# Conditioning products of a two-layer DiT as four column groups of 256 instead of two of 512, with the row turned by transposes

## The chip, the cores and the metric

One core of a Trainium2 chip. The metric is the time of one execution in device microseconds (us), as the median of several runs. Engines are called as in the profile: PE is TensorE's products, PEld its weight loads, DVE is VectorE, ACT ScalarE, POOL GpSimd, SP SyncE (whose queue issues most transfers).

## The reference, cut to what matters

A model of two layers with hybrid attention: 1024 tokens of 1024 features and 256 context rows. Every layer starts with a modulation whose three parts come from one product of a small vector with a wide matrix:

```python
def _modulate(x, cond, norm_g, w_ada, b_ada):
    mod = jax.nn.silu(cond) @ w_ada + b_ada
    shift, scale, gate = jnp.split(mod[:, None, :], 3, axis=-1)
    return rmsnorm(x, norm_g) * (1.0 + scale) + shift, gate

h, gate = _modulate(x, c, norm_g, w_ada, b_ada)
hc, gate_c = _modulate(xc, c_ctx[None, :], norm_g, w_ada, b_ada)
...
x = x + gate * (y @ w_out)
```

There are two vectors, `c` for the tokens and `c_ctx` for the context; `w_ada` is 1024 x 3072 in fp32, one for each layer. Shift and scale are wanted with the features on the partitions, the gate as a row.

## The kernel before, in words

All work on TensorE is products of 128 partitions. The large products take both factors as a high and a low part (three products each, lines L288 to L290); the conditioning is done in plain fp32.

`ada_third(wt, name, layer, third)` (from L400) computes one third of one layer's modulation: third 0 is shift, 1 is scale, 2 is gate. It runs over eight steps `kt` of 128 input features. A step loads 128 x 1024 of the matrix into a tile `wada` (SP's queue, six buffers) and makes two products on line L407. The weights on the array are `sil`, silu of the two vectors, padded with zeros to 32 columns; what streams through are the 512 columns of each half `c`. A product uses one group `g` of 32 columns of the array, and writes 32 partitions of the PSUM tile `acc[c]`. The group moves with the step, so each of the two PSUM tiles holds four partial sums, on its four groups of partitions:

```python
for c in range(2):
    g = 32 * ((kt + 2 * c) % 4)
    T_.matmul(acc[c][g:g + 32, :], sil[:, kt], w[:, c * 512:(c + 1) * 512], start=kt < 4, stop=kt >= 4)
```

ACT and DVE copy the two halves to a row in SBUF (`mrow`, L412). The four partial sums are then added up by another product with `fold`, a 128 x 2 matrix that has ones for each group's two real rows. For shift and scale the row is the weight, eight products of two columns give the features on the partitions (L433, `tps`), and DVE adds the bias into `modT` (L440) and, for scale, multiplies with the norm's weight (L443). For a gate `fold` is the weight, two products give a row (L419), DVE adds the bias `bada`, and a transfer writes it to memory (`GROW`), from where the output projection loads it.

Two of the six thirds are computed in the first stage: (layer 0, scale), while the first four blocks of x are normed (L457), turned (L481) and copied; and (layer 0, shift), between the first projections (`products`) and the turning of four more blocks (`cols_scaled`, L496). In the first of them line L488, ACT's scaling of the turned blocks into `hE`, waits for `modT`; L573 is ACT's cast of a weight `ws`. Around 65 to 150 us context columns are turned (L464, whose evictions are `hE` and `hf`, L467 to L473), queries and keys get their rope (`rope_split`: shuffle L315, POOL L316, DVE L317 and L318), and the values `vat` are projected (L656) and turned (L697); `qb` (L636) is a small bias for the first queries.

The other four thirds, in the order of `ADA_E1` = (0, gate), (1, shift), (1, scale), (1, gate), run in the second stage (`cond_gen`, from L706) beside the value projections (`main_gen`), whose weights are split into `whi` (ACT, L234) and `wlo` (DVE and POOL, L235). A `Filler` interleaves two generators: each `yield` tells how many us of TensorE's time it has issued, and after each step of the conditioning the other side may issue `FILL_E1` us. A scheduler then places the instructions of each engine; the order it gives is read from the lists under "The change".

Of the kernel before, what the change touches and what calls it, by code (L numbers as in the profile page):

```python
# [9 lines left out]
F32 = mybir.dt.float32  # L10
# [4 lines left out]
ALU = mybir.AluOpType  # L15
# [3 lines left out]
P = 128  # L19
D = 1024  # L20
NK = D // P
# [10 lines left out]
SM_COND, SM_GE, SM_GO, SM_SUB, SM_SINK, SM_LAM, SM_QG, SM_BE, SM_BO = 0, 16, 24, 32, 33, 41, 297, 300, 316  # L32
# [11 lines left out]
Q_BUFS_D, WO_V, WO_Y, YL_V = 2, 2, 5.0, 1  # L44
M_HALF = 2
POOL_MIX, POOL_Q = (0,), (8,)
# [51 lines left out]
def body(nc, tc, I, out, dbg=None):  # L98
    V, A, G, T_, SY = nc.vector, nc.scalar, nc.gpsimd, nc.tensor, nc.sync
# [11 lines left out]
    const = pool(top, "const", side="left")  # L111
# [15 lines left out]
    def s_ps():  # L127
        return psc.tile([P, 512], F32, tag="s", name="sps")

    def t_ps():  # L130
        return ptp.tile([P, 512], F32, tag="tp", name="tps")
# [5 lines left out]
    SY.dma_start(small, I["small"])  # L137
    consts = const.tile([P, P + 2], F32, name="consts")
    SY.dma_start(consts, I["ident"])
    ident, fold = consts[:, :P], consts[:, P:]  # L140
    modT = [const.tile([P, 16, 2], F32, name=f"modT{i}") for i in range(2)]
# [30 lines left out]
    GROW = spill("grow", [3, D])  # L172
# [11 lines left out]

    # ---- small helpers
    def rsqrt(v, n):
# [50 lines left out]

    # ---- interleaving of generators; what they yield is the tensor engine's time in us
    def run(gen):
# [45 lines left out]

    # ---- products
    def mm3(ps, lh, ll, rh, rl, first, last):
# [110 lines left out]

    # ---- conditioning
    def ada_third(wt, name, layer, third):  # L400
        acc = [s_ps() for _ in range(2)]
        for kt in range(NK):
            w = wt.tile([P, D], F32, tag="wada", name="wada", bufs=ADA_BUFS)
            SY.dma_start(w, I[name][kt * P:(kt + 1) * P, third * D:(third + 1) * D])
            for c in range(2):
                g = 32 * ((kt + 2 * c) % 4)
                T_.matmul(acc[c][g:g + 32, :], sil[:, kt], w[:, c * 512:(c + 1) * 512], start=kt < 4, stop=kt >= 4)  # L407
            yield 0.5
        split = (layer, third) == (0, 1)
        row = wt.tile([P, D], F32, tag="mrow", name="mrow", bufs=1)  # L410
        for c in range(2):
            (V.tensor_copy if c else A.copy)(row[:, c * 512:(c + 1) * 512], acc[c])  # L412
        if third == 2:
            b = wt.tile([2, D], F32, tag="bada", name="bada", bufs=1)
            SY.dma_start(b, I["b_gate"][layer])
            for c in range(2):
                cs_ = slice(c * 512, (c + 1) * 512)
                ps = t_ps()
                T_.matmul(ps[:2, :], fold, row[:, cs_], start=True, stop=True)  # L419
                V.tensor_tensor(b[:, cs_], ps[:2, :], b[:, cs_], ALU.add)  # L420
            if layer == 0:
                SY.dma_start(GROW[0:2], b)
            else:
                SY.dma_start(GROW[2:3], b[0:1])
        else:
            if split:
                yield 0.0
            nh = M_HALF if split else 1
            for i0 in range(0, 8, 8 // nh):
                n = 8 // nh  # L430
                ps = t_ps()
                for i in range(n):
                    T_.matmul(ps[:, 2 * i:2 * i + 2], row[:, (i0 + i) * P:(i0 + i + 1) * P], fold,  # L433
                              start=True, stop=True)

                def feat(off):
                    return small[:, off + i0:off + i0 + n].unsqueeze(2).to_broadcast([P, n, 2])

                dst = modT[layer][:, 8 * third + i0:8 * third + i0 + n]
                V.tensor_tensor(dst, ps[:, :2 * n].rearrange("p (i j) -> p i j", j=2),  # L440
                                feat((SM_BO if layer else SM_BE) + 8 * third), ALU.add)
                if third == 1:
                    V.scalar_tensor_tensor(dst, dst, 1.0, feat(SM_GO if layer else SM_GE), ALU.add, ALU.mult)  # L443
        yield 0.2
# [74 lines left out]

    # ---- even layer  # L520
    mark("start")
# [203 lines left out]

    # ---- window attention, the other queries and keys alongside
    mark("A")
# [122 lines left out]

    # ---- differential attention, the gates and the conditioning alongside
    mark("B")
# [155 lines left out]

    # ---- output projection, even; h of the odd layer
    def out_half(op, y, wo, x, gate, xn, c, kts):  # L1010
# [60 lines left out]

    # ---- odd layer
    LCH = CHUNKS[:2]
# [161 lines left out]

    # ---- neighbourhood attention, the gates alongside
    mark("D")
# [146 lines left out]

    # ---- latent attention
    mark("M")
# [92 lines left out]

    # ---- output projection, odd; final norm  # L1480
    mark("outO")
# [44 lines left out]
def layout(inp):  # L1526
    f = {k: np.asarray(v) for k, v in inp.items()}
    r = {}
# [40 lines left out]
    r["fg"] = f["final_norm_g"].reshape(1, D)  # L1569
    r["ident"] = np.concatenate([np.eye(P), np.tile(np.eye(32, 2), (4, 1))], axis=1).astype(np.float32)  # L1570
    r["flip"] = 8.0 * np.eye(P, dtype=np.float32)[::-1]
# [20 lines left out]
```

## Time and profile before

| what | us |
|---|---|
| median of 3 runs | 1714.09 |
| lowest and highest run | 1710.77 and 1715.72 |
| span of the profiled execution | 1716.7 |
| PE busy in it | 1622.0 (94%) |
| DVE, ACT, POOL busy | 1121.5, 780.7, 465.9 |
| DMA, mean over the span | 142 GB/s |

The profiled execution's own time is its span, 2.6 us above the median. A page of such a profile gives the busy time of each engine first; since PE's 94% is a mean over stages with different limits, the stages of the conditioning (from 11 us to 260 us) are shown apart in the rows below. In a row, "idle before <- releaser" names what ended the idle time just ahead of an instruction, and PEclk is the clock that TensorE was granted, as a share of full speed. A group such as "x8" holds instructions of one line that lie next to each other, with the time from the first start to the last end.

### The profile page before, as it was taken

The numbers are of one execution on the slowest core, as the hardware profiler recorded it, in microseconds if no ns is written. First come the engines' busy times: TensorE is split into PE (matmuls) and PEld (weight loads), VectorE is DVE, ScalarE is ACT, GpSimd is POOL, SyncE is SP. The second block draws the span as 40 slices with busy tenths as digits, with TensorE's granted clock in tenths as the row PEclk, the third lists the DMA queues.
The fourth block names the chain that finished last, engine by engine and source line by source line (L and its number), as shares of the span: only waits on it lengthen the run. The fifth ranks groups of instructions, "written<-read, shape, count | busy, mean of one in ns | idle before, by whom it ended". The sixth has DMA issues, their size and how long they took to land. (4 is left out here: it accounts for less than half of the span.)

```text
span 1716.7 us, 26624 instructions
## 1 busy us (share of the span) xinstructions
PE 1622.0 (94%) x9378; PEld 1359.4 (79%) x9378; DVE 1121.5 (65%) x2974; ACT 780.7 (45%) x1592; POOL 465.9 (27%) x388
## 2 busy tenths in 40 slices
PE   6988999999999989998989999999999999999997
PEld 3676668888887877887777798889788887888886
DVE  4583207878759887888677646352577666666586
ACT  4342105757646655655433323222466554545321
POOL 0252104545433222322322201120232223322110
PEclk9999999999999999999999999999999999999999
DMA  7446764243251423321754523558855345321362
GB/s 272 167 120 200 230 193 118 76 132 117 74 207 58 121 71 123 104 99 56 227 178 135 178 74 111 175 170 237 213 170 166 91 133 180 129 80 62 90 224 98
DMA packets 157155, 242.98 MB, mean 142 GB/s; under 512 B 10327, under 2 KB 103383, under 8 KB 154334
## 3 DMA queue, kind: packets, MB, share of 16 engines
q1 hardware_dynamic: 152110, 227.91, 43.5%
q10 hardware_dynamic: 4576, 11.54, 1.7%
q8 instruction: 74, 1.21, 0.3%
q0 software_dynamic: 336, 1.84, 0.3%
q14 instruction: 59, 0.48, 0.1%
HBM read 163.50 MB, written 77.74 MB: 141 GB/s over the span
## 5 line engine op out<-in xcount | busy, mean ns | idle before, releaser
L288 PE MATMUL mmps<-hE,whi 128*128 128x512 f32 (+1 forms) x408 | 148.8, 365 | 1.7 <-DVE gg L373 1.0
L290 PE MATMUL mmps<-hE,wlo 128*128 128x512 f32 (+1 forms) x408 | 147.1, 361 | 0.0
L289 PE MATMUL mmps<-hE,whi 128*128 128x512 f32 (+1 forms) x408 | 146.7, 359 | 0.0
L235 POOL TENSOR_TENSOR wlo<-wraw,whi 128x1024 fp32r<-128x1024 f32 x30 | 72.2, 2408 | 227.3 <-ACT whi L234 188.2
L896 ACT ACTIVATE sB_t<-sB_t,mB 128x1280 f32<-128x1280 f32 (+1 forms) x80 | 95.5, 1194 | 61.1 <-DVE sB_t L384 54.9
L888 PE MATMUL sps<-kb,qb 128*128 128x512 f32 (+1 forms) x416 | 106.6, 359 | 6.7 <-DVE sB_t L384 5.7
L288 PEld LDWEIGHTS mmps<-hE,whi 128*128 128x128 f32 x408 | 77.7, 191 | 13.7 <-issue 2.5
L290 PEld LDWEIGHTS mmps<-hE,wlo 128*128 128x128 f32 x408 | 77.6, 190 | 11.8 <-issue 2.5
L289 PEld LDWEIGHTS mmps<-hE,whi 128*128 128x128 f32 x408 | 77.7, 190 | 10.5 <-issue 1.7
L384 DVE TENSOR_SCALAR_CACHE_REDUCE sB_t<-sps,mB 128x512 f32<-128x512 f32 (+1 forms) x128 | 78.1, 612 | 10.9 <-PE sps L888 8.7
L888 PEld LDWEIGHTS sps<-kb,qb 128*128 128x128 f32 x416 | 68.8, 189 | 18.9 <-DVE sB_t L384 9.5
L1427 POOL TENSOR_SCALAR sM_t<-sM_t,sM 128x1280 f32<-128x1280 f32 x32 | 42.9, 1342 | 145.3 <-DVE sM L1426 113.5
L1328 POOL TENSOR_SCALAR sD_t<-sD_t,sD 128x640 f32<-128x640 f32 (+1 forms) x64 | 48.5, 779 | 104.8 <-ACT phd L213 36.9
L289 PE MATMUL mmps<-hO,whi 128*128 128x512 f32 (+1 forms) x192 | 75.2, 392 | 1.3 <-POOL hO L473 1.2
L288 PE MATMUL mmps<-hO,whi 128*128 128x512 f32 (+1 forms) x192 | 76.0, 396 | 0.0
L290 PE MATMUL mmps<-hO,wlo 128*128 128x512 f32 (+1 forms) x192 | 74.6, 389 | 0.0
L904 POOL TENSOR_SCALAR sB_t<-sB_t,cB 128x1280 f32<-128x1280 f32 (+1 forms) x20 | 23.4, 1172 | 180.7 <-DVE cB L902 67.0
L763 ACT ACTIVATE sA_t<-sA_t,mA 128x640 f32<-128x640 f32 (+2 forms) x80 | 59.6, 745 | 25.1 <-DVE sA_t L384 24.2
L213 ACT CAST phm<-tps 128x512 fp32r<-128x512 f32 x80 | 45.7, 584 | 51.4 <-PE tps L1454 51.2
L773 POOL TENSOR_SCALAR sA_t<-sA_t,eA 128x640 f32<-128x640 f32 (+2 forms) x80 | 57.6, 742 | 42.1 <-DVE eA L771 27.4
L316 POOL TENSOR_TENSOR rot<-rot,csE 128x512 f32<-128x512 f32 x26 | 36.1, 1392 | 120.0 <-DVE rot L315 108.8
L214 DVE TENSOR_TENSOR plm<-tps,phm 128x512 fp32r<-128x512 f32 x80 | 54.3, 689 | 19.6 <-ACT phm L213 19.4
(438 smaller groups left out, 5334.2 us busy)
## 6 DMA issues: line engine op xcount, KB each, us to landing
wraw<-w_e SPq DMA_DIRECT2D x26, 512.0 KB, 3.9
wada<-w_ada_e SPq DMA_DIRECT2D x24, 512.0 KB, 5.9
wada<-w_ada_o SPq DMA_DIRECT2D x24, 512.0 KB, 4.5
wraw<-w_o SPq DMA_DIRECT2D x22, 512.0 KB, 4.5
qb<-qk SPq DMA_DIRECT2D x76, 128.0 KB, 3.1
qd_t<-qd SPq DMA_DIRECT2D x32, 256.0 KB, 4.6
qk<-hl SPq DMA_DIRECT2D x10, 512.0 KB, 3.1
vb<-vh SPq DMA_DIRECT2D x20, 256.0 KB, 2.9
```

What stands on the lines that cost most here:

```text
L213: A.copy(dst_hi, src)
L214: (V if psum else lo_eng()).tensor_tensor(dst_lo, src, f32(dst_hi), ALU.subtract)
L235: lo_eng().tensor_tensor(lo[:, j], raw[:, :width], f32(hi[:, j]), ALU.subtract)
L288: T_.matmul(ps, lh, rh, start=first, stop=False)
L289: T_.matmul(ps, lh, rl, start=False, stop=False)
L290: T_.matmul(ps, ll, rh, start=False, stop=last)
L384: V.tensor_scalar(dst, ps, -scale, prev, ALU.mult, ALU.min, accum_out=acc)
L763: A.activation(St[:, :nl + L], St[:, :nl + L], AF.Exp, bias=mx, scale=-1.0, accum_out=ssum[:, i:i + 1])
L773: G.tensor_scalar(Ps[i][:, :nl + L], Ps[i][:, :nl + L], e[:, i:i + 1], 1.0, ALU.mult, ALU.mult)
L888: T_.matmul(ps[:, :n], Q[:, t, hl, i * P:(i + 1) * P], K[:, t, c0:c0 + n], start=hl == 0, stop=hl == 1)
L896: A.activation(St[:, :ncol], St[:, :ncol], AF.Exp, bias=mx, scale=-1.0, accum_out=s0g[:, si:si + 1] if t == 0 else ssum)
L1328: G.tensor_scalar(Ps[i][:, :w_], Ps[i][:, :w_], ssum[:, i:i + 1], 1.0, ALU.mult, ALU.mult)
```

## The change

One PSUM tile of 256 columns takes the place of two of 512. In every step four products of 256 columns are made, one for each group of the array's columns, and a group keeps its quarter of the output through all eight steps. So there are no partial sums over groups: partitions 32g and 32g + 1 hold the two vectors' values for the columns 256g to 256g + 255. `fold` goes away. For shift and scale, ACT copies the 128 x 256 row, two transposes turn it (L426 of the new numbering), and one addition of DVE with a four-dimensional view takes the two wanted columns of each group. For a gate, `bada` is a 128 x 256 tile, zeroed by POOL and filled by four small transfers; DVE adds it straight from PSUM, and four transfers write the quarters to `GROW`. Line numbers after the change are lower by up to 15: L407 becomes L404, L288 to L290 become L286 to L288, L457 becomes L449, L481 L473, L496 L488, L636 L628.

```diff
-M_HALF = 2
...
-    consts = const.tile([P, P + 2], F32, name="consts")
-    SY.dma_start(consts, I["ident"])
-    ident, fold = consts[:, :P], consts[:, P:]
+    ident = const.tile([P, P], F32, name="consts")
+    SY.dma_start(ident, I["ident"])
...
     def ada_third(wt, name, layer, third):
-        acc = [s_ps() for _ in range(2)]
+        acc = s_ps()[:, :256]
         for kt in range(NK):
             w = wt.tile([P, D], F32, tag="wada", name="wada", bufs=ADA_BUFS)
             SY.dma_start(w, I[name][kt * P:(kt + 1) * P, third * D:(third + 1) * D])
-            for c in range(2):
-                g = 32 * ((kt + 2 * c) % 4)
-                T_.matmul(acc[c][g:g + 32, :], sil[:, kt], w[:, c * 512:(c + 1) * 512], start=kt < 4, stop=kt >= 4)
+            for g in range(4):
+                T_.matmul(acc[32 * g:32 * g + 32, :], sil[:, kt], w[:, g * 256:(g + 1) * 256],
+                          start=kt == 0, stop=kt == NK - 1)
             yield 0.5
-        split = (layer, third) == (0, 1)
-        row = wt.tile([P, D], F32, tag="mrow", name="mrow", bufs=1)
-        for c in range(2):
-            (V.tensor_copy if c else A.copy)(row[:, c * 512:(c + 1) * 512], acc[c])
+        row = wt.tile([P, 256], F32, tag="mrow", name="mrow", bufs=1)
         if third == 2:
-            b = wt.tile([2, D], F32, tag="bada", name="bada", bufs=1)
-            SY.dma_start(b, I["b_gate"][layer])
-            for c in range(2):
-                cs_ = slice(c * 512, (c + 1) * 512)
-                ps = t_ps()
-                T_.matmul(ps[:2, :], fold, row[:, cs_], start=True, stop=True)
-                V.tensor_tensor(b[:, cs_], ps[:2, :], b[:, cs_], ALU.add)
-            if layer == 0:
-                SY.dma_start(GROW[0:2], b)
-            else:
-                SY.dma_start(GROW[2:3], b[0:1])
+            b = wt.tile([P, 256], F32, tag="bada", name="bada", bufs=1)
+            G.memset(b, 0.0)
+            for g in range(4):
+                SY.dma_start(b[32 * g:32 * g + 2], I["b_gate"][layer][:, g * 256:(g + 1) * 256])
+            V.tensor_tensor(row, acc, b, ALU.add)
+            for g in range(4):
+                cs_ = slice(g * 256, (g + 1) * 256)
+                if layer == 0:
+                    SY.dma_start(GROW[0:2, cs_], row[32 * g:32 * g + 2])
+                else:
+                    SY.dma_start(GROW[2:3, cs_], row[32 * g:32 * g + 1])
         else:
-            if split:
+            A.copy(row, acc)
+            if (layer, third) == (0, 1):
                 yield 0.0
-            nh = M_HALF if split else 1
-            for i0 in range(0, 8, 8 // nh):
-                n = 8 // nh
-                ps = t_ps()
-                for i in range(n):
-                    T_.matmul(ps[:, 2 * i:2 * i + 2], row[:, (i0 + i) * P:(i0 + i + 1) * P], fold,
-                              start=True, stop=True)
...
-                dst = modT[layer][:, 8 * third + i0:8 * third + i0 + n]
-                V.tensor_tensor(dst, ps[:, :2 * n].rearrange("p (i j) -> p i j", j=2),
-                                feat((SM_BO if layer else SM_BE) + 8 * third), ALU.add)
...
+            ps = t_ps()
+            for i in range(2):
+                T_.transpose(ps[:, i * P:(i + 1) * P], row[:, i * P:(i + 1) * P], ident)
...
+            dst = modT[layer][:, 8 * third:8 * third + 8].rearrange("p (g i) j -> p g i j", i=2)
+            V.tensor_tensor(dst, ps[:, :256].rearrange("p (i g r) -> p g i r", i=2, g=4)[:, :, :, 0:2],
+                            feat((SM_BO if layer else SM_BE) + 8 * third), ALU.add)
...
```

Three places show how the order moves. The first is TensorE's order at the end of the first third, before and after: the products of the conditioning (`sps<-wada,sil`, an fp32 product counts once here), the turning of x (`tps<-consts,xt`), and the row's own end (`tps<-consts,mrow`).

```order
L407 MATMUL sps<-wada,sil 32x512
L481 MATMUL tps<-consts,xt 128x128 x8
L407 MATMUL sps<-wada,sil 32x512 x3
L481 MATMUL tps<-consts,xt 128x128 x4
L407 MATMUL sps<-wada,sil 32x512 x4
L433 MATMUL tps<-consts,mrow 128x2 x8
L288 MATMUL mmps<-hE_134,ws_145 128x512
```

```order
L404 MATMUL sps<-wada,sil 32x256 x4
L473 MATMUL tps<-consts,xt 128x128 x8
L404 MATMUL sps<-wada,sil 32x256 x4
L473 MATMUL tps<-consts,xt 128x128 x8
L404 MATMUL sps<-wada,sil 32x256 x11
L426 MATMUL tps<-consts,mrow 128x128 x2
L286 MATMUL mmps<-hE_134,ws_145 128x512
```

The last two steps of the third stand together in both; three products of the step ahead now stand with them, and two transposes stand where eight products stood.

The second place is TensorE's order in the second stage, where (1, shift) ends, before and after. L288 to L290 (after: L286 to L288) are value projections; the first ones of 256 columns take a new weight, whose low half is `wlo`.

```order
L290 MATMUL mmps<-hE_134,wlo 128x512
L407 MATMUL sps<-wada,sil 32x512 x9
L288 MATMUL mmps<-whi,hE_134 128x256 x2
L407 MATMUL sps<-wada,sil 32x512 x2
L433 MATMUL tps<-consts,mrow 128x2 x4
L407 MATMUL sps<-wada,sil 32x512
L289 MATMUL mmps<-wlo,hE_134 128x256
```

```order
L288 MATMUL mmps<-hE_134,wlo 128x512
L404 MATMUL sps<-wada,sil 32x256 x13
L286 MATMUL mmps<-whi,hE_134 128x256 x2
L404 MATMUL sps<-wada,sil 32x256 x4
L287 MATMUL mmps<-wlo,hE_134 128x256
```

Nine products and then three became thirteen and four of half the width, and the half of the fold products that stood ahead of the first use of `wlo` is gone from there.

The third place is DVE's order near 72 us, around the copy of `qb`. L200 to L203 are the steps of a reciprocal square root, L457 (after: L449) scales two blocks of context, L315 (L313) is the first shuffle of the rope.

```order
L202 SCALAR_TENSOR_TENSOR rst<-rst,rv 128x2
L636 COPY qb<-tps 128x8
L203 SCALAR_TENSOR_TENSOR rsy<-rst,rsy 128x2
L457 TENSOR_SCALAR xt<-xt,rsy 128x1024 x2
L315 STREAM_SHUFFLE rot<-qf 128x512
```

```order
L200 SCALAR_TENSOR_TENSOR rst<-rst,rv 128x2
L201 SCALAR_TENSOR_TENSOR rsy<-rst,rsy 128x2
L449 TENSOR_SCALAR xt<-xt,rsy 128x1024 x2
L628 COPY qb<-tps 128x8
L313 STREAM_SHUFFLE rot<-qf 128x512
```

The copy of `qb` moves from ahead of the last correction step and the two scalings to behind them, right ahead of the shuffle.

## Rows read from the trace of the kernel before

In the tables by stage the columns are start and end of a stretch, its length, the busy us of each engine named (number of its instructions), PEclk, the share of time in which the DMA engines were busy, and GB/s; with all engines these are PE, PEld, DVE, ACT, POOL, with line L407 alone PE and PEld.

**Rows 1.** Table by stage, all engines, third and fourth stretch.
```profile
64.60:154.90 90.30, 80.36 (x435) 66.44 (x434) 66.72 (x105) 37.60 (x70) 43.64 (x30) 0.94 0.38 112
154.90:260.20 105.30, 103.95 (x655) 70.64 (x655) 19.01 (x35) 12.99 (x27) 5.99 (x3) 1.00 0.70 218
```
**Rows 2.** Waits of PE from 64.6 to 154.9; total us, times, longest.
```profile
PE tps L697 <- ACT vat L656: 4.1, 2, 3.8
PE tps L464 <- ACT hf L470: 3.6, 1, 3.6
```
**Rows 3.** Table by stage, line L407 alone, first, second and fourth stretch.
```profile
11.30:30.30 19.00, 9.09 (x32) 1.11 (x32) 1.00 0.74 278
30.30:64.60 34.30, 8.42 (x32) 1.15 (x32) 0.95 0.72 267
154.90:260.20 105.30, 29.73 (x128) 4.60 (x128) 1.00 0.70 218
```
**Rows 4.** Line L407; duration in ns (min/median/max), first and last start, form.
```profile
L407 PE MATMUL sps<-wada,sil x192: 592/592/1063, 11.3 to 256.9; 128*32 128x512 f32 x192
```
**Rows 5.** Timeline, PE around a lone step; start us, duration us, instruction.
```profile
160.76 1.05 PE L407 MATMUL sps<-wada,sil 128*32 128x512 f32 x4
...
162.09 0.28 PE L288 MATMUL mmps<-whi,hE 128*128 128x256 f32 x1
162.21 0.28 PE L289 MATMUL mmps<-wlo,hE 128*128 128x256 f32 x1
```
**Rows 6.** Timeline, PE and DVE, 198 to 206.
```profile
198.63 2.76 PE L407 MATMUL sps<-wada,sil 128*32 128x512 f32 x18
...
205.08 0.36 PE L289 MATMUL mmps<-wlo,hE 128*128 128x256 f32 x1 [0.32 <-DVE wlo L235]
...
198.82 0.76 DVE L315 STREAM_SHUFFLE rot<-mmps 128x512 f32<-128x512 f32 x1
...
200.97 2.82 DVE L318 TENSOR_TENSOR rr<-rr,rot 128x512 f32<-128x512 f32 x1 [0.83 <-POOL rot L316]
203.72 1.21 DVE L235 TENSOR_TENSOR wlo<-wraw,whi 128x1024 fp32r<-128x1024 f32 x1
```
**Rows 7.** Timeline, PEld, PE and ACT, end of the first third.
```profile
25.50 0.16 PEld L407 LDWEIGHTS sps<-wada,sil 128*32 128x32 f32 x8 [0.17 <-issue]
25.50 1.06 PE L407 MATMUL sps<-wada,sil 128*32 128x512 f32 x8
...
27.28 1.95 PE L433 MATMUL tps<-consts,mrow 128*128 128x2 f32 x16 [0.71 <-ACT mrow L412]
...
27.12 1.05 ACT L573 CAST ws<-wraw 128x1024 fp32r<-128x1024 f32 x1
29.59 3.79 ACT L488 ACTIVATE hE<-raw,modT 128x512 fp32r<-128x512 f32 x6 [1.43 <-DVE modT L443]
```
**Rows 8.** Timeline, PE, the first cluster of the first third.
```profile
11.33 1.89 PE L407 MATMUL sps<-wada,sil 128*32 128x512 f32 x2 [11.33 <-DMA wada<-w_ada_e]
```
**Rows 9.** Timeline, PE, end of the second third.
```profile
62.46 0.60 PE L496 MATMUL tps<-consts,xt 128*128 128x128 f32 x4
62.89 1.84 PE L433 MATMUL tps<-consts,mrow 128*128 128x2 f32 x16
```
**Rows 10.** Timeline, PE, end of the last gate third.
```profile
258.33 1.88 PE L419 MATMUL tps<-mrow,consts 128*2 128x512 f32 x4
```
**Rows 11.** The view of the first group, just behind the wait for vat.
```profile
147.20:151.00 3.80, 3.76 (x19) 3.77 (x20) 1.60 (x4) 1.28 (x4) 2.23 (x1) 0.55 0.69 150
```
**Rows 12.** Timeline, PE and DVE, start of the second third.
```profile
46.02 0.38 PE L496 MATMUL tps<-consts,xt 128*128 128x128 f32 x2
...
45.07 2.07 DVE L457 TENSOR_SCALAR xt<-xt,rsy 128x1024 f32<-128x1024 f32 x3
```
**Rows 13.** Timeline, DVE, 71 to 76.
```profile
71.96 2.02 DVE L203 SCALAR_TENSOR_TENSOR rsy<-rst,rsy 128x2 f32<-128x2 f32 x1
...
75.35 0.73 DVE L315 STREAM_SHUFFLE rot<-qf 128x512 f32<-128x512 f32 x1
```

More of the change, by code (lines that the diff above doesn't have):

```diff
@@ L427, in ada_third @@
                 yield 0.0
-            nh = M_HALF if split else 1
-            for i0 in range(0, 8, 8 // nh):
-                n = 8 // nh
-                ps = t_ps()
-                for i in range(n):
-                    T_.matmul(ps[:, 2 * i:2 * i + 2], row[:, (i0 + i) * P:(i0 + i + 1) * P], fold,
-                              start=True, stop=True)
-                def feat(off):
-                    return small[:, off + i0:off + i0 + n].unsqueeze(2).to_broadcast([P, n, 2])
-                dst = modT[layer][:, 8 * third + i0:8 * third + i0 + n]
-                V.tensor_tensor(dst, ps[:, :2 * n].rearrange("p (i j) -> p i j", j=2),
-                                feat((SM_BO if layer else SM_BE) + 8 * third), ALU.add)
-                if third == 1:
-                    V.scalar_tensor_tensor(dst, dst, 1.0, feat(SM_GO if layer else SM_GE), ALU.add, ALU.mult)
+            ps = t_ps()
@@ new lines, in ada_third, with feat @@
+            for i in range(2):
+                T_.transpose(ps[:, i * P:(i + 1) * P], row[:, i * P:(i + 1) * P], ident)
+            def feat(off):
+                return small[:, off:off + 8].rearrange("p (g i) -> p g i", i=2).unsqueeze(3).to_broadcast([P, 4, 2, 2])
+            dst = modT[layer][:, 8 * third:8 * third + 8].rearrange("p (g i) j -> p g i j", i=2)
+            V.tensor_tensor(dst, ps[:, :256].rearrange("p (i g r) -> p g i r", i=2, g=4)[:, :, :, 0:2],
+                            feat((SM_BO if layer else SM_BE) + 8 * third), ALU.add)
@@ L444, in ada_third @@
+            if third == 1:
+                V.scalar_tensor_tensor(dst, dst, 1.0, feat(SM_GO if layer else SM_GE), ALU.add, ALU.mult)
         yield 0.2
@@ L1569, in layout @@
     r["fg"] = f["final_norm_g"].reshape(1, D)
-    r["ident"] = np.concatenate([np.eye(P), np.tile(np.eye(32, 2), (4, 1))], axis=1).astype(np.float32)
+    r["ident"] = np.eye(P, dtype=np.float32)
     r["flip"] = 8.0 * np.eye(P, dtype=np.float32)[::-1]
```

## The prediction

> **What bounds the kernel now.** I read the table by stage first (busy time of each engine per stretch), because the change touches only the 260 us in which the six thirds of the conditioning are computed. In the second stage, 154.9 to 260.2, TensorE is busy 103.95 of 105.3 us at full clock while the DMA engines stand at a share of 0.70 [rows 1]: what TensorE is spared there is time, until something else comes late. From 64.6 to 154.9 TensorE is busy 80.36 of 90.3 [rows 1], and the table of waits says why: it stands 3.6 us for ACT's hf and 3.8 us for ACT's vat, ends of chains over other engines [rows 2]. Time won before such a wait is kept only if the chain moves forward with it.
>
> Next the same windows for the products' line alone: 9.09 us busy in the first third, 8.42 in the second, 29.73 in the four of the second stage [rows 3]. Then the shape of one step. A fp32 product of 512 columns is two records (the table by line counts 192 for 96 products), of 592 ns each [rows 4]. A lone step, two products in two column groups, takes 1.05 us [rows 5]. In a stretch of nine products, 18 records take 2.76 us [rows 6]: three rounds of the four groups are six passes in a row, so a pass comes (2.76 − 0.59) / 5 = 0.434 us after the one before it in its group, and 1.05 is 2 × 0.434 + 0.18. The row that carries the forecast is 25.50: eight records, four products in four groups, two of them in each PSUM tile, take 1.06, no longer than a lone step [rows 7]. Four groups run side by side; a lone step today uses half of the array's columns.
>
> **The products.** After the change a step is four products of 256 columns in four groups, two passes each. A pass half as wide costs half, 0.217, so a lone step is 2 × 0.217 + 0.18 = 0.61. The bounds are no gain (1.05) and 0.52; I take 0.61 because the fixed 0.18 is the drain of the last pass. In the second stage the order listing has 23 lone steps and three longer stretches of 13, 15 and 9 products. The fullest group of these has 4, 4 and 3 products, that is 8, 8 and 6 passes: 1.92, 1.92 and 1.48. Together 23 × 0.61 + 5.3 = 19.4 for 29.73: **−10.3**.
>
> In the second third (layer 0, shift) there are nine clusters, 9 × 0.61 = 5.5 for 8.42: −2.9. In the first third (layer 0, scale), 1.89 of the 9.09 us lie in the first cluster, which waits for its second weight transfer [rows 8]; of the 7.2 left up to 2.9 could go, but the steps follow transfers at 278 GB/s and a DMA share of 0.74 [rows 3]. I take −1.9, two thirds; ends 0 and −2.9.
>
> **The folds.** A shift or scale third ended in eight fold products, 1.84 us; four transposes beside them start 0.43 before the next work, so two cost 0.22 [rows 9]. In the second stage two thirds: 2 × 1.84 − 0.44 = 3.2, **−3.2**. In the second third −1.6. A gate third ended in two fold products, four records, 1.88 us [rows 10]; they vanish, twice: **−3.8**. The rest of the gate's tail (a POOL memset, eight small transfers in place of two) is read by nothing before the next stage; it costs nothing as long as SP's queue, which runs ahead there, is not the one that is late. [...]
>
> In the first third the tail stands on the path: after the last product ends (25.50 + 1.06 = 26.56) ACT starts on hE at 29.59 [rows 7], 3.03 us later, through row copies, 1.95 of folds and the additions. With one copy, two transposes and the additions this chain is about 1.4 us; ACT also has the weight CAST of 1.05 in its queue, which started 0.56 after the products' end [rows 7] and would end at +1.6. I take +1.45 for +3.03: **−1.6**, ends −1.2 and −1.8.
>
> **What is late next.** (a) Around 198.6 to 205.1 TensorE's products are cover for a chain of another kind. It starts with DVE's shuffle at 198.82, goes over POOL and DVE's addition of 2.82 us at 200.97 to the low half of a weight, DVE 203.72 for 1.21, on which TensorE's L289 waits; that wait is only 0.32 us today [rows 6]. Ahead of L289 there are now (by the order listing) 13 products, 1.92, two projections, 0.25 by their spacing of 0.12 [rows 5] and a switch, and a lone step, about 3.0 us in all from 198.63. The chain doesn't change, so L289 still comes 6.45 after 198.63: a wait of some 3.5 us, **+3.2** over today's.
>
> (b) A wait of that length has a price behind it. After the 3.8 us for vat [rows 2] the granted clock is 0.55, near the lower of its two levels (1.2 of 2.4 GHz), for the 3.8 us that follow, though TensorE is busy throughout [rows 11]: 0.45 × 3.8 = 1.7 us lost. I add **+1.6** for the same behind (a); the lower end is 0, if the wait stays clearly shorter.
>
> (c) In the second stage the first two steps wait for their weights' transfers already, and the second of them wins nothing: **+0.4**. More, shorter clusters mean three more changes between products and projections: **+0.3**. (d) In the second third the transposes at 46.02 stand right behind DVE's scaling of xt, three in a row from 45.07 [rows 12]: some 0.8 of the gain turns into a wait there, and one more switch costs 0.2: **+1.0**. (e) Near 72 us the order on DVE changes too. Today the small copy qb is ahead of a correction step that took 2.02 us at 71.96 and two scalings, and the first rope shuffle starts at 75.35 [rows 13]; after the change these three stand ahead of qb, so the shuffle may follow its input up to 2.4 us sooner, or the qb wait is only moved. I take **−1.0**, ends 0 and −2.4.
>
> **The sum.** First third −1.9 − 1.6 = −3.5; second third −2.9 − 1.6 + 1.0 = −3.5; (e) −1.0; second stage −10.3 − 3.2 − 3.8 + 3.2 + 1.6 + 0.4 + 0.3 = −11.8. Together −19.8. The profiled execution has a span of 1716.7, so 1696.9 on its scale; it stands 2.6 above the median of 1714.1, and by that median the forecast is **1694.3 us**. All that follows 260 us keeps its order, so the shift is carried to the end.
>
> **Rivals.** *1. The loads can't hide.* Eight weight loads are all done within 0.16 us at the start of the 1.06-us cluster in which the products run, on all 128 rows [rows 7]. Were each group's load instead to wait for the products before it, a lone step would grow by some 0.07 (half of 0.16), 48 steps: +3.4, 1697.7. The Trainium skill, "TensorE: Matmul & The Clock Gate", Part 3 (What overlaps and what doesn't), has a rule of that kind: weight loads run under running products only where the row group differs, and here all four products use every row group. The row named speaks against it. Chance 0.08.
>
> *2. The early gain is swallowed.* If the chains behind hf and vat [rows 2] hang on weight transfers and casts that don't move, the −7.0 of the first two thirds and (e) come back as longer waits at 92, 96 or 147 us: about −12, 1702. For it: the waits exist and are long. Against it: the inputs of those chains are products of the stretch before, and ACT is busy 37.60 of the 90.3 us [rows 1]. Chance 0.13.
>
> *3. Slower: one bank, one group at a time.* The four groups now write the same PSUM tile, where today each tile takes two at a time. If groups in one tile took turns, the 192 products would be 384 passes of 0.217, 83 us, plus 48 tails of 0.18, about 92 for today's 47.2 [rows 3]; less 10 for the folds that is some +35, **1749**. It decides as soon as fewer than two groups run at once. Against it: in the 25.50 cluster two groups share each tile and still no time is lost [rows 7]. Chance 0.03.
>
> *4. It does nothing.* If the second stage can't be fed faster (it moves 218 GB/s now, against 278 in the first third [rows 1, 3]), or new waits like (a) take the rest, the gain is under 5 us: 1709 and above. 218 × 105.3 / 278 = 83 us of transfers at that rate, below the 93 that I forecast. Chance 0.04.
>
> **How the numbers follow.** The forecast's own case has 0.68. With the gain of (a) kept and (b) absent it is 1689.5, with (e) in full 1688; with nothing from (e), the folds and the first third at their poor ends 1699. Another 0.04 goes below 1687. Rivals 1 and 2 are inside a range that reaches from 1687 to 1703; outside stay below 1687, rivals 3 and 4, and a little of 2: under 0.2. A difference of 0.3%, 5.1 us, is about what a measurement of this kernel can tell from no change. Faster by more than that are the forecast, the cases below it, and rivals 1 and 2: 0.93; same 0.04; slower 0.03.
>
> **What would show it.** A lone step of eight records at 0.6 us, the products' line at about 19.4 us in the second stage and about 32 in all for 47.2; the lines of the folds gone; ACT's hE about 1.45 us after the last product of the first third; a wait of TensorE of 3 to 4 us for DVE's low half where 0.32 stood, with a fallen clock behind it; the stage near 93.5 us. A lone step at 1 us or more, or the sum of the waits at 92, 96 and 147 grown by 5 us or more, would make the forecast wrong.

## The result

| | median us | runs | span of the profiled execution |
|---|---|---|---|
| before | 1714.9 | 1710.77 to 1717.07, 4 runs | 1716.7 |
| after | 1693.2 | 1691.89 to 1694.84, 4 runs | 1692.6 |

The ratio is 0.9867 with a 95% interval of 0.9842 to 0.9893. The forecast was 1694.3 us, the range 1687 to 1703.

The table by stage shows where the time went. In the kernel after, the second third ends at 57.80 (before: 64.60), the second stage begins with the first step at 146.62 (before: 154.92). Columns as in [rows 1]; the second fence is the products' line L404 (before: L407) alone, as in [rows 3].

```profile
57.80:146.30 88.50, 79.10 (x436) 65.70 (x434) 69.02 (x105) 39.01 (x71) 45.37 (x31) 0.96 0.39 113
146.30:238.90 92.60, 89.57 (x746) 69.76 (x747) 15.25 (x32) 11.38 (x25) 6.29 (x4) 0.98 0.77 248
```

```profile
27.50:57.80 30.30, 5.72 (x64) 1.39 (x64) 0.94 0.80 301
146.30:238.90 92.60, 20.83 (x256) 6.12 (x256) 0.98 0.77 248
```

The second stage took 105.3 us before and takes 92.6; its products take 20.83 us of TensorE in place of 29.73, and the DMA engines now move 248 GB/s there against 218. TensorE is no longer busy all of it. What it waits for, in total us, times and the longest:

```profile
PE mmps L287 <- DVE wlo L233: 1.6, 1, 1.6
PE sps L404 <- DMA wada<-w_ada_e: 1.0, 1, 1.0
PE sps L404 <- DMA wada<-w_ada_o: 0.9, 1, 0.9
```

The timeline of a lone step in that stage, and of the wait for wlo (start, duration, instruction):

```profile
149.30 0.64 PE L404 MATMUL sps<-wada,sil 128*32 128x256 f32 x8
...
187.65 0.62 PE L404 MATMUL sps<-wada,sil 128*32 128x256 f32 x2 [0.92 <-DMA wada<-w_ada_o]
189.84 0.55 PE L287 MATMUL mmps<-wlo,hE 128*128 128x256 f32 x1 [1.57 <-DVE wlo L233]
```

A step is 0.64 us where it was 1.05 [rows 5]. The wait for DVE's low half, 0.32 before [rows 6], has grown, as forecast, but to 1.57; 0.92 more lies ahead of it, in a wait for a transfer. The chain to that low half on DVE, which answers to [rows 6]:

```profile
183.59 0.75 DVE L313 STREAM_SHUFFLE rot<-mmps 128x512 f32<-128x512 f32 x1
...
188.48 1.21 DVE L233 TENSOR_TENSOR wlo<-wraw,whi 128x1024 fp32r<-128x1024 f32 x1
```

From the shuffle to the product that waits it is 6.25 us (183.59 to 189.84), as before (198.82 to 205.08). And the granted clock behind the wait, by stretch:

```profile
187.00:190.00 3.00, 0.78 (x3) 0.33 (x4) 3.00 (x3) 0.62 (x1) 1.01 (x1) 0.91 0.50 195
190.00:193.00 3.00, 3.00 (x15) 3.00 (x16) 0.29 (x1) 0.00 (x0) 0.00 (x0) 0.52 0.45 93
193.00:196.00 3.00, 3.00 (x27) 3.00 (x27) 0.42 (x1) 0.37 (x1) 0.00 (x0) 1.00 0.24 82
```

TensorE was busy 0.78 of the 3 us up to 190; in the 3 us after it, busy throughout, it had a clock of 0.52, near its lower level, and did 15 products where the next 3 us hold 27.

The end of the first third, PE and ACT, which answers to [rows 7]:

```profile
24.08 1.50 PE L404 MATMUL sps<-wada,sil 128*32 128x256 f32 x22
26.06 0.44 PE L426 MATMUL tps<-consts,mrow 128*128 128x128 f32 x2 [0.48 <-ACT mrow L421]
...
25.90 1.05 ACT L565 CAST ws<-wraw 128x1024 fp32r<-128x1024 f32 x1
27.01 5.02 ACT L480 ACTIVATE hE<-raw,modT 128x512 fp32r<-128x512 f32 x8
```

The last product ends at 25.58; ACT's hE follows at 27.01, 1.43 us later, where 3.03 stood, and right behind the weight CAST.

**How leads are read below.** The work behind the second stage is the same in all kernels, and up to the mark TensorE does it in the same order in all but x2, so I take one late instruction as a mark: the last transpose of the window attention, whose start stands as the second time in the row of its line. Before and after:

```profile
L785 PE MATMUL tps<-consts,sA_t x336: 270/272/329, 282.1 to 489.1; 128*128 128x128 f32 x168
```

```profile
L777 PE MATMUL tps<-consts,sA_t x336: 270/272/330, 260.9 to 468.1; 128*128 128x128 f32 x168
```

The lead is 489.1 - 468.1 = 21.0 us, and the same 21.2 at its first transpose: so all of it was made before the window attention, in the stages of the change and in the stretch between them. The lead at 290 us, of which the expectations speak, is read at the first transpose; it differs from the one at the last by under 1 us in every kernel but x2.

### The profile page after: what moved, and what is told of

The parts are those of the page before. It is cut to its first block, busy times and chain, and to the rows that moved or that the text cites. A ratio compares the mean times of both kernels' runs of the same rounds, so it can differ in the third digit from the quotient of the medians.

```text
span 1692.6 us, 26893 instructions
## 1 busy us (share of the span) xinstructions
PE 1599.0 (94%) x9506; PEld 1355.1 (80%) x9506; DVE 1117.1 (66%) x2964; ACT 779.0 (46%) x1590; POOL 468.1 (28%) x390
## 3 DMA queue, kind: packets, MB, share of 16 engines
q8 instruction: 75, 1.23, 0.3%
## 5 line engine op out<-in xcount | busy, mean ns | idle before, releaser
L286 PE MATMUL mmps<-hE,whi 128*128 128x512 f32 (+1 forms) x408 | 148.8, 365 | 1.7 <-DVE gg L371 1.0
L288 PE MATMUL mmps<-hE,wlo 128*128 128x512 f32 (+1 forms) x408 | 146.7, 360 | 0.0
L286 PEld LDWEIGHTS mmps<-hE,whi 128*128 128x128 f32 x408 | 77.7, 190 | 12.8 <-issue 2.5
L288 PEld LDWEIGHTS mmps<-hE,wlo 128*128 128x128 f32 x408 | 77.4, 190 | 10.3 <-issue 0.8
L286 PE MATMUL mmps<-hO,whi 128*128 128x512 f32 (+1 forms) x192 | 75.8, 395 | 0.0
L288 PE MATMUL mmps<-hO,wlo 128*128 128x512 f32 (+1 forms) x192 | 74.5, 388 | 0.0
```

Source lines behind the costliest of these rows:

```text
L286: T_.matmul(ps, lh, rh, start=first, stop=False)
L288: T_.matmul(ps, ll, rh, start=False, stop=last)
```

## The experiments

Times are medians beside the kernel before on the same chip; leads are against the mark at 489.1.

| run | median us | before, same chip | ratio (95%) | mark | lead |
|---|---|---|---|---|---|
| x1_products_only | 1694.7 | 1718.0 | 0.9865 (0.9836 to 0.9893) | 478.3 | 10.8 |
| x2_tails_only | 1704.7 | 1718.0 | 0.9919 (0.9891 to 0.9946) | 487.4 | 1.7 |
| x3_start_only | 1701.0 | 1718.0 | 0.9907 (0.9877 to 0.9937) | 480.6 | 8.5 |
| x4_second_raw | 1686.3 | 1718.0 | 0.9815 (0.9786 to 0.9844) | 463.6 | 25.5 |
| x5_before_again | 1716.2 | 1716.5 | 0.9999 (0.9977 to 1.0021) | 491.6 | -2.5 |
| x6_old_products_new_tails | 1701.2 | 1716.5 | 0.9913 (0.9886 to 0.9941) | 482.4 | 6.7 |
| x7_after_again | 1694.0 | 1716.5 | 0.9861 (0.9818 to 0.9903) | 472.2 | 16.9 |
| x8_before_second_raw | 1718.1 | 1716.5 | 1.0012 (0.9982 to 1.0041) | 491.0 | -1.9 |
| x9_two_groups | 1701.2 | 1720.4 | 0.9886 (0.9859 to 0.9913) | 476.9 | 12.2 |
| x10_second_raw_again | 1691.5 | 1720.4 | 0.9836 (0.9818 to 0.9853) | 462.7 | 26.4 |
| x11_after_third | 1693.0 | 1720.4 | 0.9845 (0.9822 to 0.9868) | 469.3 | 19.8 |

One kernel's lead varies by some 4 us between profiles (after: 21.0, 16.9, 19.8; before: 0, -2.5). Between the mark and the end lie 1212 to 1230 us, in an order that has nothing to do with the leads; that part is the subject of x5.

### The steps alone: x1

```diff
-            ps = t_ps()
-            for i in range(2):
-                T_.transpose(ps[:, i * P:(i + 1) * P], row[:, i * P:(i + 1) * P], ident)
+            for i in range(n):
+                f = i0 + i
+                g = f // 2
+                T_.matmul(ps[:, 2 * i:2 * i + 2], row[:, (f % 2) * P:(f % 2 + 1) * P], ident[:, 32 * g:32 * g + 2],
+                          start=True, stop=True)
```

The gate's tail goes back to products in the same way (four of 256 columns).

> The four 256-column products stay; the ends of the thirds are the old ones again (eight 128x2 products for shift and scale, four 256-column products for a gate, in place of two transposes and none). Own theory (TensorE's time is the time in these stages, steps and tails add up): the steps alone are worth 10.3 + 2.9 + 1.9 = 15.1 us, less what the wait for wlo takes, so 12 to 15 below the kernel before, 1700 to 1703, with a lone step of 0.64. Rival (the steps were hidden behind weight transfers, the gain is in the tails): within 5 us of before, 1710 or more.

The lead is 10.8, a little under the 12 to 15 expected; the rival falls. (By the median it is 23.3; the rest comes behind the mark, see x5.) In the timeline the wait for the new weight has another name here: it stands behind 26 records of the conditioning, ahead of the high half's first product, and 20 more records follow before the low half is used:

```profile
191.03 1.91 PE L404 MATMUL sps<-wada,sil 128*32 128x256 f32 x26
195.24 0.50 PE L286 MATMUL mmps<-whi,hE 128*128 128x256 f32 x2 [2.30 <-ACT whi L232]
195.68 1.49 PE L404 MATMUL sps<-wada,sil 128*32 128x256 f32 x20
```

TensorE waits 2.30 for ACT's high half instead of DVE's low half: shorter steps uncover the weight's arrival, here its other half. x6 will show that the shorter tails alone uncover it too.

### The tails alone: x2 and x6

x2 was meant to keep the steps as wide as before and only drop the folds:

```diff
-            for g in range(4):
-                T_.matmul(acc[32 * g:32 * g + 32, :], sil[:, kt], w[:, g * 256:(g + 1) * 256],
+            for g in range(2):
+                T_.matmul(acc[32 * g:32 * g + 32, :], sil[:, kt], w[:, g * 512:(g + 1) * 512],
                           start=kt == 0, stop=kt == NK - 1)
```

> Two products of 512 columns per step in two fixed column groups, as wide as before, but no partial sums: no folds, four transposes for shift and scale, none for a gate. Own theory: a lone step stays at 1.05, the tails are worth 3.2 + 1.6 + 3.8 + 1.6 less 0.6 for two more transposes three times, so 8 to 10 below before, 1705 to 1707. Rival (tails hidden, steps carry all): within 3 us of before, 1712 or more.

The lead at the mark is 1.7: neither theory. Two things lie behind it. The timeline of its PE shows what I had changed without meaning to:

```profile
228.60 1.05 PE L404 MATMUL sps<-wada,sil 128*32 128x512 f32 x4
...
236.64 3.62 PE L404 MATMUL sps<-wada,sil 128*32 128x512 f32 x14
240.79 4.48 PE L404 MATMUL sps<-wada,sil 128*32 128x512 f32 x18
```

Lone steps are 1.05, as expected. But each half now keeps its column group, so steps that stand next to each other queue in the same two groups: nine products take 4.48 us, where the turning groups of the kernel before take 2.76 [rows 6], and seven take 3.62. The turn of the groups from step to step had a use: it lets neighbouring steps run side by side. In the second stage the products take 35.23 us here and 29.73 before [rows 3], 5.5 more.

The other thing has nothing to do with the conditioning. In this kernel alone the order of TensorE behind the second stage is another. At the first 256-column projections behind the stage, which stand at 264.57 before and at 259.85 here, the lead is still 4.7; the other 3 us go in the window attention, where one wait is longer by 2.2 than before (the first line is x2, the second the kernel before), with a clock of 0.50 over the 3 us behind it:

```profile
304.61 0.79 PE L752 MATMUL sps<-ka,qa 128*128 128x256 f32 x2 [3.12 <-DVE mA L384]
```

```profile
305.86 0.50 PE L759 MATMUL sps<-ka,qa 128*128 128x256 f32 x2 [0.91 <-DVE mA L386]
```

So x2 doesn't speak against the 8 to 10 of own theory: 4.7 and the 5.5 that the queueing costs are 10.2, an estimate from these two numbers. x6 keeps the turn, and the tails of the changed kernel:

```diff
-            for g in range(4):
-                T_.matmul(acc[32 * g:32 * g + 32, :], sil[:, kt], w[:, g * 256:(g + 1) * 256],
-                          start=kt == 0, stop=kt == NK - 1)
+            for c in range(2):
+                g = 32 * ((kt + 2 * c) % 4)
+                T_.matmul(accs[c][g:g + 32, :], sil[:, kt], w[:, c * 512:(c + 1) * 512], start=kt < 4, stop=kt >= 4)
...
+        acc = accs[1][:, :256]
```

> The old products of 512 columns, turning through the four groups as before, with the new tails exactly (one copy of 256 columns, two transposes, no product for the gates). Left out: the sum of the four partial rows, and three quarters of the row; only a quarter of the outputs of the products is read. Own theory (steps and tails are each time of TensorE and add up): the lead at 290 us is that of the changed kernel less that of the products alone, 21.2 - 11.1 = 10 us, with lone steps at 1.05 and pairs of steps still side by side. Rival (they don't add up; what x2_tails_only lost was no matter of steps that follow each other in one group): 0 to 4 us, as there.

The lead is 6.7, nearer to own theory's 10 than to the rival's 4, and short of it by 3.3, within the spread between profiles. Of the 3.3 the timeline names 2.1: the steps are as wide as before, and yet TensorE waits for the low half, 2.42 where it was 0.32. The tails, too, had covered that weight's arrival:

```profile
201.01 0.36 PE L287 MATMUL mmps<-wlo,hE 128*128 128x256 f32 x1 [2.42 <-DVE wlo L233]
```

Steps and tails together are 10.8 + 6.7 = 17.5, and the changed kernel has 16.9 to 21.0. The sum holds the wait for that weight twice (2.30 in x1, 2.42 here), which the changed kernel pays once. They add up as far as these profiles can tell.

### What a step wins: x9

```diff
-            for g in range(4):
-                T_.matmul(acc[32 * g:32 * g + 32, :], sil[:, kt], w[:, g * 256:(g + 1) * 256],
-                          start=kt == 0, stop=kt == NK - 1)
+            for g in range(4):
+                p0 = 32 * (g % 2 + 2 * (kt % 2))
+                T_.matmul(accs[g // 2][p0:p0 + 32, :256], sil[:, kt], w[:, g * 256:(g + 1) * 256],
+                          start=kt < 2, stop=kt >= NK - 2)
```

> The four products of 256 columns and the new tails, but a step uses two column groups (two products after each other in each), and the groups change from one step to the next, as before the change. Left out: the sum of the two partial rows, and half of the row. Own theory (what a step wins is the two more groups at work at the same time, not the smaller product): a lone step takes 4 x 0.217 + 0.18 = 1.05 again, and the lead at 290 us falls from about 20 to about the 7 of x6_old_products_new_tails. Rival (products of 256 columns are cheaper by themselves, or a step is bound by its loads): a lone step near 0.64 and a lead of 15 us or more.

The same four products in two groups, by the timeline:

```profile
155.21 1.06 PE L405 MATMUL sps<-wada,sil 128*32 128x256 f32 x8
```

1.06 for 0.64: the smaller product by itself wins nothing, the two more groups at work win it all. The lead, 12.2, is between what the two theories said. The 5.5 us over x6 have two places. The first projection starts at 26.86, in x6 at 29.72: in the first third the steps stand together here, and 26 records in a row take 1.93 (there 8 records take 1.07). And no wait for wlo stands in this kernel's table of waits, since DVE makes the low half between the shuffle and the other steps of the rope (192.07, with the shuffle at 191.43), and not behind them as in x6 (199.65, with the shuffle at 194.76):

```profile
192.07 1.21 DVE L233 TENSOR_TENSOR wlo<-wraw,whi 128x1024 fp32r<-128x1024 f32 x1
```

So the lead at the mark doesn't price the two groups alone; the row of the lone step does.

### Is the early gain carried: x3

Only (layer 0, scale) and (layer 0, shift) run in the new form.

```diff
+START_NEW = ((0, 1), (0, 0))
...
+        if (layer, third) in START_NEW:
+            yield from ada_four(wt, name, layer, third)
+            return
```

> Only the two thirds of the first stage run in the new form, the four of the second stage as before. Own theory (a gain before 64 us is carried through the waits at 92, 96 and 147 us): 7 to 8.5 below before, 1706.5 to 1708. Rival (the chains behind those waits don't move and swallow it): 1711 or more, with the sum of these waits grown by 5 us or more.

The lead is 8.4 at the first transpose of the window attention (273.7) and 8.5 at the last. The waits on the way, from 55 to 150 us:

```profile
PE tps L740 <- ACT vat L699: 4.3, 2, 3.8
PE tps L507 <- ACT hf L513: 2.6, 1, 2.6
PE tps L507 <- DVE hf L515: 1.8, 2, 0.9
```

Before, hf by ACT was 3.6, vat 4.1 [rows 2], and the third of these waits was this one:

```profile
PE tps L464 <- DVE hf L472: 1.5, 1, 1.5
```

Their sum is 8.7 where it was 9.2, so they haven't grown: the chains behind them moved forward with TensorE, and the rival falls. The median, however, is 17 us below before, not 7 to 8.5; half of that comes behind the mark.

### The new wait: x4, x8, x10

```diff
-        W2 = Weights(st, "left", hi_bufs=1, raw_bufs=1, maxk=2)
+        W2 = Weights(st, "left", hi_bufs=1, raw_bufs=2, maxk=2)
```

> The changed kernel with two raw buffers instead of one for the value projections' weights in the second stage, so that the second half's transfer, cast and low half no longer stand behind the first half's. Own theory: the wait for wlo near 190 us (1.57) and the fallen clock behind it (1.6) go: 2.5 to 4 below the changed kernel, 1689 to 1691, no stretch of the second stage at a clock of 0.6 or less. Rival (the stage is fed by transfers, so the wait only moves to wada): within 1 us of the changed kernel, 1692 to 1694, waits for DMA wada of 3 us or more in the stage.

The lead is 25.5 against 16.9 to 21.0, more than the 2.5 to 4 expected, and the median lies below the 1689 to 1691. The wait and the low clock are gone, and the waits for wada in the stage are 0.9 and 0.2, so the rival falls; the stretches of x4 that answer to the ones above:

```profile
186.00:189.00 3.00, 3.00 (x29) 2.45 (x28) 2.56 (x1) 0.41 (x1) 2.01 (x1) 1.00 0.29 114
189.00:192.00 3.00, 3.00 (x29) 2.45 (x29) 1.45 (x3) 0.86 (x3) 0.00 (x0) 1.00 0.25 54
```

With one raw buffer the second half's transfer is issued at 180.35, as POOL is done with the buffer (177.93 and 2.40), and DVE makes the low half only behind the rope, at 188.48. With two, DVE makes it ahead of the rope's shuffle, which starts at 183.58:

```profile
178.82 2.57 DVE L233 TENSOR_TENSOR wlo<-wraw,whi 128x1024 fp32r<-128x1024 f32 x1 [1.48 <-ACT whi L232]
```

So the second weight is ready early, and TensorE goes from one weight to the next without a stop. The same edit in the kernel before:

> The kernel before with two raw buffers for the value projections' weights, as x4_second_raw for the changed one (where the lead at 290 us was 25.7 against 21.2). Own theory (the wait that x4 takes away is made by the change; before, products covered it up to 0.32 us): at most 1.5 us at 290 us. Rival (the single buffer cost as much before the change, hidden in other waits): 3 us or more at 290 us.

Its mark is 491.0, within the 489.1 and 491.6 of the kernel before: no gain there, so this wait came with the change. The pair was run again on one chip, with the third profile of the changed kernel:

> x4_second_raw again, beside the changed kernel on the same chip, for its lead. Own theory: 3 to 7 us below x11_after_third in the median, and again no wait for wlo and no fallen clock near 190 us. Rival (x4's time was a lucky set of late transfers): within 2 us.

> The changed kernel again, for the comparison with x10 and for a third profile: its lead at 290 us is 17 to 21 us as in the first two, with the wait for wlo near 190 us at 1 to 2 us and a clock of 0.5 to 0.6 in the 3 us behind it; its time 20 to 24 us below the kernel before.

The marks are 462.7 and 469.3, so the edit is worth 6.6 us at the mark once more; x11 has the wait again, 2.70 us, and this stretch behind it:

```profile
190.80:193.80 3.00, 2.93 (x14) 2.96 (x15) 0.52 (x1) 0.00 (x0) 0.00 (x0) 0.50 0.38 77
```

But the medians are 1691.5 and 1693.0, 1.6 apart, under the 3 to 7 expected and within the rival's 2. In the two profiled executions 2.7 of the 6.6 us were lost behind the mark (1227.4 for 1224.7); where the others lost the rest isn't shown. It is ahead of both kernels in each comparison, of the changed one by 6.9 us (1686.3 against the 1693.2 of another comparison) and 1.6; the intervals against before, 0.9786 to 0.9844 and 0.9818 to 0.9853, overlap those of the changed kernel.

### Behind the mark: x5 and x7

> The kernel before, unchanged, with a profile of its own on the chip of the other runs. Asked: where the 3 to 13 us come from that the four runs so far stand below their own lead at 290 us, all of them between 800 and 1480 us. Theory A (chance and chip: transfers of the later stages land at other times from one run to the next): this profile differs from the first one of before by several us in that stretch too, in the same places (around 860, 1215, 1331 and 1432 us). Theory B (the shift itself: a kernel that comes to these places earlier finds its transfers done): this profile agrees with the first one within 2 us at 290, 800 and 1480 us.

> The changed kernel, unchanged, on the same chip. Theory A of x5 (chance and chip): its lead over x5 at the end is its lead at 290 us, 21 us, within 4. Theory B (the shift): the lead grows behind 800 us, by 3 to 13 us as in the four others.

Neither theory holds as put. x5 ends 0.4 us behind the first profile, near what B said, but it is 2.5 behind at the mark, and its waits behind 780 us are others. Of the first profile, and of x5:

```profile
PE tps L464 <- DVE hf L472: 4.0, 4, 3.0
```

```profile
PE tps L464 <- DVE hf L472: 1.4, 4, 0.4
PE sps L1418 <- DMA kp<-kpe: 2.2, 1, 2.2
```

One wait is shorter by 2.6, another of 2.2 is new, and they nearly cancel. x7, which B wanted to gain behind the mark, lost there, in a profiled execution of 1703.7 us while its other runs took 1689.6 to 1694.9. Two of its waits that the first profile of the changed kernel doesn't have:

```profile
PE sps L286 <- DMA kn<-ckv: 2.9, 1, 2.9
PE sps L1410 <- issue: 2.4, 1, 2.4
```

The part behind the mark took 1227.6, 1225.5 and 1224.4 us in the three profiles of a kernel with the old conditioning throughout, 1224.5, 1229.7 and 1224.7 in the changed one, and 1217.2 and 1227.4 in two profiles of one and the same kernel (x4 and x10). x1, x3 and x6 took 1214.4, 1216.3 and 1217.1. Part of what varies is the clock: over the 20 runs of the kernel before beside x5, time goes with the mean granted clock of the run, from 1709.1 us at 0.990 to 1729.1 at 0.979. The 13 profiles show the same: their part behind the mark goes from 1211.8 us at a mean clock of 0.992 (x2) to 1229.7 at 0.982 (x7). Whether the clock makes the time or other waits make both isn't shown. Why some kernels stay low there, run after run, though the edits don't touch what stands behind the mark, stays open.

## Why the prediction was right

**The sum** said -19.8; the three leads are 21.0, 16.9 and 19.8. The rest of the program passed it on, and the time came out 1.1 us from the forecast. That it came so near is luck in part: one kernel's lead varies by 4 us, the part behind the mark by more, and of the steps below the products and the first third gave less than forecast, the others more. By its steps, in the first profile:

- *First third*, -3.5 predicted. The first projection starts at 27.79 for 30.37: -2.6. The tail is right to 0.02 (1.43 us, forecast 1.45). The steps were worth only 0.6: the last product ends 0.98 sooner, and the first had started 0.35 sooner. The bound of 0 was nearer than the -1.9 that I took.
- *Second third*, -3.5 predicted. From 30.37 to 64.60 it took 34.23, now 30.01 from 27.79: -4.2. Products -2.7 (5.72 for 8.42), close to the 2.9; the 0.8 that I charged for a wait on DVE's xt wasn't paid.
- *(e), near 72 us*, -1.0. The lead grows from 6.8 at the end of the second third to 8.3 at the first step of the second stage: -1.5. The way was the one forecast for the first 0.9 of it: the shuffle of [rows 13] starts 7.7 sooner (67.67), and so does TensorE's first transpose behind the wait for hf (84.25 for 91.92, the lines below).
- *Second stage*, -11.8. From 8.3 to 21.2: -12.9. The products were the term most off, -8.9 for -10.3: a step is 0.64, not 0.61, which over 23 lone steps is half of the miss, and the stretch of 13 took 2.25, not 1.92. (a) gave +2.2 (1.57 and 0.92, less 0.32) for +3.2. Its chain took as long as forecast; TensorE had more ahead of it, the longer stretch of 13 and a step that a transfer broke in two. In x7 and x11 the wait was 2.70, with 0.27 for a transfer ahead of it. (b) was right in size: 0.48 x 3.0 = 1.4 us for 1.6; but that the length of the wait brings it on isn't borne out, as the last section shows. (c) was not seen: one wait of 1.0 in place of two that made 1.0. With 6.9 for the folds (7.70 us of them before, 0.82 of transposes now) these make -12.2; 0.7 is left without a term. The eight small transfers of a gate take 2.5 us of SP's queue (1.25 and 1.23); no wait of TensorE in the stage names them.

The wait for hf of (e), before and after:

```profile
91.92 0.44 PE L464 MATMUL tps<-consts,xt 128*128 128x128 f32 x2 [3.56 <-ACT hf L470]
```

```profile
84.25 0.69 PE L456 MATMUL tps<-consts,xt 128*128 128x128 f32 x2 [2.77 <-ACT hf L462]
```

**The rivals.** Rival 1 (loads can't hide) would have made a step 0.68; it is 0.64, midway to the 0.61. But a stretch of 22 records, six passes in the fullest group, takes 1.50 at the end of the first third: 6 x 0.217 + 0.20, where a step is 2 x 0.217 + 0.20. The fixed part is the same with 22 loads as with eight, so the loads add nothing; they still take 0.16 us in the trace of the changed kernel, as in [rows 7]:

```profile
22.49 0.16 PEld L404 LDWEIGHTS sps<-wada,sil 128*32 128x32 f32 x8 [0.17 <-issue]
22.49 0.64 PE L404 MATMUL sps<-wada,sil 128*32 128x256 f32 x8
```

The rule of the Trainium skill, "TensorE: Matmul & The Clock Gate", Part 3 (What overlaps and what doesn't), by which loads overlap with running products only in another row group, doesn't describe this trace: all eight use all 128 rows. Rival 2 (the early gain swallowed) is answered by x3 and by the lead of 8.3 in the changed kernel. Rival 3 (one bank, one group at a time) falls with 0.64 for four groups in one PSUM tile, and x9 shows what it costs if only two work at once. Rival 4 had a point in one place: the second stage has come closer to its transfers (248 GB/s for 218, two waits for wada of 1.0 and 0.9 us), but TensorE is still busy 89.57 of its 92.6 us.

## What to carry to other kernels

A product that uses a narrow strip of the array's columns wants neighbours in the other strips: cut the free side until all four strips are at work in every step, and let the output's layout follow, so that partial sums need no further product. When such work shrinks in a stage that TensorE bounds, ask what it was covering: here a weight's arrival, with the wait itself and then a low clock behind it. A second buffer took both away, 6.6 us at the mark on one chip, of which 1.6 were left in the median. And before reading a few us in a long program, take a mark right behind the change, see that the work up to it keeps its order, and profile the old kernel twice.

## What the runs showed of the hardware

The granted clock can have its price behind a wait: three profiles of the changed kernel show 0.50 to 0.60 over 3 us, with TensorE busy for 2.60 to 3.00 of them, behind waits of 1.57 (with 0.92 just ahead of it) to 2.70 us. I had expected it behind 3.5. But it isn't paid behind each such wait: behind x6's 2.42 the clock stayed at 1.00, though TensorE was busy for only 0.59 of the 3 us ahead, less than the 0.78 of the changed kernel:

```profile
198.00:201.00 3.00, 0.59 (x4) 0.02 (x1) 3.00 (x3) 0.89 (x2) 1.18 (x1) 1.00 0.33 127
201.00:204.00 3.00, 2.99 (x25) 3.00 (x26) 0.47 (x1) 0.00 (x0) 0.00 (x0) 1.00 0.40 81
```

Behind x1's 2.30 it stayed at 1.00 as well (195 to 198 us). What tells these cases apart isn't shown.

And neighbouring steps in the same column group queue, while in others they don't: nine products in two groups took 4.48 us, in four 2.76.
